# A row of a load split over 126 and 2 partitions: in the sixth load instead of the second

## The chip, the core and the metric

The kernel runs on one core of a Trainium2 chip. The metric is the device time of one execution in microseconds, taken over several executions. The engines that matter here are DVE (VectorE), ACT (ScalarE) and SP (SyncE), and the 16 DMA engines of the core, which move data between HBM and SBUF.

## The reference: what is computed

A softmax with temperature 2 over the last axis of a tensor of 16 x 1024 x 512 float32 values (33.55 MB in, 33.55 MB out):

```python
x_scaled = x / 2.0
x_max = np.max(x_scaled, axis=-1, keepdims=True)
exp_x = np.exp(x_scaled - x_max)
return exp_x / np.sum(exp_x, axis=-1, keepdims=True)
```

## The kernel before

The 16,384 rows of 512 values are dealt to 128 partitions, so each partition holds 128 rows of 2 KB. They are handled in ten tiles, t0 to t9, of 3, 7, 13 and seven times 15 rows per partition (`PLAN`, lines 11 to 14). One tile is one load and one store: each of the 128 partitions reads or writes one contiguous piece of 2 KB times the rows of the tile, so 6, 14, 26 and seven times 30 KB. A tile is computed in chunks of 3 to 5 rows.

All data lies in one SBUF buffer, the arena, of 98 rows per partition. Tiles t0 to t7 have places of their own; t8 and t9 take the places of t0 to t3, so their loads must wait until those tiles have been stored. Data is transformed in place.

- **Loads** (`issue_loads`, lines 98 to 114). SP issues the load of t0 (line 105). ACT issues those of t1 to t7 one after the other on its own DMA queue, without a wait: t1 ahead of the program's opening barrier, in the entry block (line 229), t2 to t7 behind the barrier. One tile, number `SPREAD`, is loaded by three DMAs (lines 108 to 112) where the others are loaded by one (line 114): all rows but the last over 128 partitions, then the last row for partitions 0 to 125, then the last row for partitions 126 and 127. The loads of t8 and t9 come later on the same queue, between ACT's computations (line 190), when the stores of t0 to t2, and of t3, have landed.
- **DVE** takes for each chunk the negated maximum (`do_max`, line 118), which waits for the tile's load: for 48 counts of its semaphore where the tile was loaded by three DMAs, for 16 otherwise (line 123). Two chunks later it forms the reciprocal of the sum (line 127) and multiplies the chunk with it, in one instruction for t1 to t3 (line 131) and row by row elsewhere (line 138). DVE's order is written out by hand: maximum of chunk k, then reciprocal and product of chunk k-2 (lines 149 to 153).
- **ACT** computes exp(0.5 x - max) row by row with the sum beside it (line 176; in a loop at line 211 for t6 to t9).
- **SP** issues the store of a tile when its last chunk is multiplied (line 158), in order of the tiles, and at the end waits for all stores (line 162).

The loads of t1 to t9 stand in one DMA queue (q10, ACT's) and the stores, with the load of t0, in another (q1, SP's). Both use the same 16 DMA engines. The lines that issue the loads and wait for them:

```python
elif t == SPREAD:
    r = tiles[t][1] - 1
    for p, q, lo, hi in ((0, P, 0, r), (0, 126, r, r + 1), (126, P, r, r + 1)):
        nc.scalar.dma_start(
            out=sb(t)[p:q, lo:hi], in_=dram(xf, t)[p:q, lo:hi]
        ).then_inc(ld[t], 16)
else:
    nc.scalar.dma_start(out=sb(t), in_=dram(xf, t)).then_inc(ld[t], 16)
...
)._wait_ge(ld[t], 48 if t == SPREAD else 16).then_inc(s_max, 1)
```

## Time and profile before

| | |
|---|---|
| median of 6 runs | 160.03 us (159.96 to 160.27) |
| the profiled execution | 160.17 us |
| its span, first to last instruction | 158.8 us |
| DVE busy | 131.4 us, 83% of the span |
| ACT busy | 94.4 us, 59% of the span |
| moved by DMA | 67.13 MB, 423 GB/s over the span |
| time of DMA packets, as a share of 16 engines' span | 50.4% (SP's queue) + 48.6% (ACT's queue) |

The span leaves out 1.37 us of the profiled execution's time, which lie around it. Times within the span are counted from its first instruction. A DMA is cut into packets, and each packet stands in the trace with its start, its length, its bytes and its queue; a packet of 4 bytes is the finishing write with which one DMA engine reports that its part of a DMA is done. "Landing" is the moment at which the last such report has reached the semaphore.

### The profile page before, as it was taken

The numbers are of one execution on the slowest core, as the hardware profiler recorded it, in microseconds if no ns is written. First come the engines' busy times: TensorE is split into PE (matmuls) and PEld (weight loads), VectorE is DVE, ScalarE is ACT, GpSimd is POOL, SyncE is SP. The second block draws the span as 40 slices with busy tenths as digits, with TensorE's granted clock in tenths as the row PEclk, the third lists the DMA queues.
The fourth block names the chain that finished last, engine by engine and source line by source line (L and its number), as shares of the span: only waits on it lengthen the run. The fifth ranks groups of instructions, "written<-read, shape, count | busy, mean of one in ns | idle before, by whom it ended". The sixth has DMA issues, their size and how long they took to land.

```text
span 158.8 us, 621 instructions
## 1 busy us (share of the span) xinstructions
DVE 131.4 (83%) x155; ACT 94.4 (59%) x257; POOL 0.2 (0%) x4
## 2 busy tenths in 40 slices
DVE  0466799999999999999999999994999479999100
ACT  0369187746784595668848697666566809664000
POOL 0000000000000000000000000000000000000000
DMA  7989999999998999999999999999999999999996
GB/s 283 441 365 429 439 430 441 433 406 414 451 430 387 448 462 424 441 420 449 418 441 418 449 418 449 418 449 410 457 410 457 410 457 410 457 410 449 418 449 263
DMA packets 3026, 67.13 MB, mean 423 GB/s; under 512 B 336, under 2 KB 336, under 8 KB 720
## 3 DMA queue, kind: packets, MB, share of 16 engines
q1 hardware_dynamic: 1584, 34.34, 50.4%
q10 hardware_dynamic: 1440, 32.77, 48.6%
q14 instruction: 2, 0.02, 0.0%
HBM read 33.55 MB, written 33.55 MB: 423 GB/s over the span
## 4 chain that ended last, share of the span: by engine, by line
DMA 53%; DVE 38%; issue 0%
DMA arena<-in_x_dram 39%; DVE stats L118 18%; DMA out_dram<-arena 14%; DVE arena L131 13%; DVE arena L138 7%; DVE recip L127 1%
## 5 line engine op out<-in xcount | busy, mean ns | idle before, releaser
L118 DVE TENSOR_REDUCE stats<-arena 128x5 f32<-128x2560 f32 (+2 forms) x27 | 72.2, 2676 | 15.0 <-DMA arena<-in_x_dram 15.0
L176 ACT ACTIVATE arena<-arena,stats 128x512 f32<-128x512 f32 x68 | 48.2, 710 | 23.4 <-DVE stats L118 23.4
L211 ACT ACTIVATE arena<-arena,stats x60 | 42.5, 709 | 21.3 <-ACTq L203 21.3
L138 DVE TENSOR_SCALAR arena<-arena,recip 128x512 f32<-128x512 f32 x93 | 38.6, 482 | 0.7
L131 DVE TENSOR_TENSOR arena<-arena,recip 128x2560 f32<-128x2560 f32 (+2 forms) x8 | 19.9, 2492 | 0.3
L176 ACT ACTIVATION_READ_ACCUMULATOR arena<-arena,stats 128x1 f32 x68 | 12.7, 187 | 0.0
L211 ACT ACTIVATION_READ_ACCUMULATOR arena<-arena,stats x60 | 11.2, 186 | 0.0
L127 DVE RECIPROCAL recip<-stats 128x5 f32<-128x5 f32 (+2 forms) x27 | 4.8, 177 | 0.0
L171 ACT ACT_TABLE_LOAD x1 | 1.3, 1283 | 5.7 <-issue 5.7
L252 POOL MEMSET const-uint8-127<- 128x1 uint8 x1 | 0.1, 103 | 0.0
L252 POOL MEMSET const-bfloat16-1.0<- 128x1 bf16 x1 | 0.1, 102 | 0.0
L252 POOL MEMSET const-float32-0.0<- 128x1 f32 x1 | 0.1, 99 | 0.2 <-issue 0.2
L252 POOL MEMSET const-float32-1.0<- 128x1 f32 x1 | 0.1, 99 | 0.0
## 6 DMA issues: line engine op xcount, KB each, us to landing
arena<-in_x_dram ACTq DMA_DIRECT2D x7, 3840.0 KB, 47.0
out_dram<-arena SPq DMA_DIRECT2D x7, 3840.0 KB, 22.4
arena<-in_x_dram ACTq DMA_DIRECT2D x1, 3328.0 KB, 14.2
out_dram<-arena SPq DMA_DIRECT2D x1, 3328.0 KB, 21.3
out_dram<-arena SPq DMA_DIRECT2D x1, 1792.0 KB, 17.5
arena<-in_x_dram ACTq DMA_DIRECT2D x1, 1536.0 KB
arena<-in_x_dram SPq DMA_DIRECT2D x1, 768.0 KB, 6.2
out_dram<-arena SPq DMA_DIRECT2D x1, 768.0 KB, 15.1
```

Source lines behind the costliest of these rows:

```text
L118: nc.vector.reduce_max(out=stats[:, b : b + c], in_=arena[:, a : a + c], axis=mybir.AxisListType.X, negate=True,)._wait_ge(ld[t], 48 if t ...
L127: nc.vector.reciprocal(out=recip[:, b : b + c], in_=stats[:, b : b + c])._wait_ge(s_exp, k + 1).then_inc(s_rec, 1)
L131: nc.vector.tensor_mul(out=arena[:, a : a + c], in0=arena[:, a : a + c], in1=recip[:, b : b + c].unsqueeze(2).to_broadcast([P, c, D]),)._w ...
L138: ins = nc.vector.tensor_scalar_mul(out=arena[:, a + r], in0=arena[:, a + r], scalar1=recip[:, b + r : b + r + 1],)
L171: nc.scalar.preload_act_table(mybir.ActivationFunctionType.Exp)
L176: ins = nc.scalar.activation(out=arena[:, a + r], in_=arena[:, a + r], func=mybir.ActivationFunctionType.Exp, bias=stats[:, b + r : b + r ...
L211: ins = nc.scalar.activation(out=data, in_=data, func=mybir.ActivationFunctionType.Exp, bias=stat, scale=0.5, accum_out=stat,)
L252: nc = _bacc.Bacc("TRN2", target_bir_lowering=False, num_devices=1)
```

## The change

```diff
-SPREAD = 1
+SPREAD = 5
```

The second load (t1, 7 rows per partition, 14 KB) becomes one DMA over 128 partitions. The sixth load (t5, 15 rows, 30 KB) becomes three: 14 rows (28 KB) over 128 partitions, then the last row over partitions 0 to 125, then the last row over partitions 126 and 127. The waits on the two semaphores change with it: 16 for t1, 48 for t5. On ACT two DMA issues move from the entry block, ahead of the barrier, to behind the issue of t4's load. No instruction of DVE, SP, PE or POOL changes its place.

## The prediction

> **What bounds the kernel now.** I first read the head of the page: span, engines, the slices, the DMA queues.

> ```profile
> span 158.8 us, 621 instructions
> DVE 131.4 (83%) x155; ACT 94.4 (59%) x257; POOL 0.2 (0%) x4
> ...
> DMA  7989999999998999999999999999999999999996
> ...
> DMA packets 3026, 67.13 MB, mean 423 GB/s; under 512 B 336, under 2 KB 336, under 8 KB 720
> ...
> q1 hardware_dynamic: 1584, 34.34, 50.4%
> q10 hardware_dynamic: 1440, 32.77, 48.6%
> ```

> The DMA engines are busy in every slice, and the two queues' shares sum to 99.0%: 157.2 us of packets on each of 16 engines. That is the bound; DVE has 27 us to spare. The chain of waits ends in DMA too:

> ```profile
> 58.69 22.37 DMA out_dram<-arena
> ...
> 81.08 46.98 DMA arena<-in_x_dram
> ...
> 128.09 2.82 DVE stats L118
> ```

> The 47 us of t9's load are mostly time in a queue, not a price. So I read where DVE waits for loads (timeline of DVE; in brackets the idle time ahead):

> ```profile
> 9.16 3.95 DVE L118 TENSOR_REDUCE stats<-arena 128x4 f32<-128x2048 f32 x2 [1.23 <-DMA arena<-in_x_dram]
> ...
> 16.87 2.82 DVE L118 TENSOR_REDUCE stats<-arena 128x5 f32<-128x2560 f32 x1 [2.37 <-DMA arena<-in_x_dram]
> ...
> 63.51 2.81 DVE L118 TENSOR_REDUCE stats<-arena 128x5 f32<-128x2560 f32 x1
> ...
> 109.95 2.82 DVE L118 TENSOR_REDUCE stats<-arena 128x5 f32<-128x2560 f32 x1 [1.99 <-DMA arena<-in_x_dram]
> ...
> 128.09 2.82 DVE L118 TENSOR_REDUCE stats<-arena 128x5 f32<-128x2560 f32 x1 [3.26 <-DMA arena<-in_x_dram]
> ```

> These are t1, t2, then t5 (its first chunk, no wait), t8 and t9. DVE is ahead of the loads again from 107.96 on.

> Last, the trace's packet records. They don't name the DMA engine, but on one engine a packet begins 4 ns before the one ahead of it ends, so they link into 16 rows. What they show:

> - From about 1.3 us to its end no engine is idle, but for a hole of 0.35 us at 45.3 and one of some 0.5 us at 140, one engine each. The 16 rows end between 157.58 and 158.32; the last report lands at 158.78.
> - One packet is one partition's piece: 1138 ns for 30 KB, 987 for 26 KB, 535 for 14 KB, 460 for 12 KB, 84 for 2 KB (80 from start to start). So 2 KB inside a long piece costs (1138 - 987)/2 = 75 ns.
> - A DMA over 128 partitions gives each engine 8 packets and one finishing write. ACT's queue has 1440 packets = 9 whole DMAs x 144, 128 single rows, and 16 finishing writes for the 126 and the 2 rows together: 126 rows on 14 engines, 9 each, and 2 on two of them. **Two engines get nothing of the split row.** They are the two that begin latest: at 7.65 they finish t1's 12 KB pieces (the others 6.93 to 7.41) and go straight on to t2; the fourteen take 9 rows and finish at 7.66 to 8.26.
> - Where both queues hold work, an engine takes them in turn, one packet of each, whatever the sizes.

> **The change, part by part** (against the profiled 160.17).

> *t1 in one piece.* The two engines have 8 x 75 = 0.60 us more: 7.65 becomes 8.25. The fourteen have 8 x 75 instead of 9 x 80 + 9 ns of finishing: 0.60 - 0.73 = 0.13 less, so the last at 8.26 becomes 8.13. t1 is complete at the same time.

> *t2.* The two engines ended it at 15.91 and 16.02, now 16.5 and 16.6; the fourteen (last 16.41) now 16.3. The load is complete 0.2 later; DVE waits there, so its first chunk of t2 moves from 16.87 to 17.05. DVE runs without a wait from there to 107.96, so stores t2 to t5 go out 0.2 later. The 1.99 us wait for t8 swallows it.

> *t5 in three pieces.* The long pieces lose 8 x 75 = 0.60 on all engines, and the fourteen gain 0.73. So **every engine's sum is what it was**: two engines +0.60 - 0.60, fourteen -0.13 + 0.13.

> *Order of the queues around t5.* Here stores run beside loads, and a row of 2 KB takes a turn like a piece of 30 KB. On a typical engine t5 was loaded at 55.08, and t2's store (26 KB pieces, first at 45.20) ended at 61.44. After: the eighth long piece (start 52.96 before) ends near 53.4, 0.73 earlier; four store pieces are done by then. Four remain and alternate with t5's finishing write and the first three rows: 53.4 + 4 x 0.99 + 3 x 0.08 = 57.6. Then the store queue is empty, and six rows follow bare, 0.5: t5 complete at 58.1, landing near 58.5 by the 0.4 us that other loads take from finishing write to report. DVE takes t5 at 63.7: 5.2 us of cover. If that cover were gone, each us would delay t4's store.

> *The next store.* t3's store is issued at 58.69, now 58.9. On engines busy with loads the first packet of a store came 3.69 (issue 14.54, packet 18.23), 4.5 (26.20, 30.71) and 3.56 us (41.64, 45.20) behind its issue. By that it begins at 62.5 to 62.8; before, behind t2's, at 62.3 to 62.6. As the engines never idle, the same bytes are moved by then, so t6's load stands where it stood too. From there on everything repeats: t8 and t9 land at 109.9 and 128.1.

> *ACT.* Three issues took 1.36 us ahead of the barrier; one long issue took 0.39. Behind the barrier the six issues (2.65 to 5.65) become eight, about 0.9 longer. If the barrier opens 0.9 sooner, nothing moves; if not, the table load (1.28) ends at 7.86, and the first exp at 7.97 still finds ACT free (its 1.01 us of idle time is the cover). Every long load is queued long before its turn. Both ends: zero.

> *The end.* The last store is issued at 147.40. The first packet of a DMA on idle engines came 1.02 behind its issue (SP's load at 0.00), so it could begin at 148.4; the last engine takes it up at 149.22. So t9's landing may be **0.8 us later before the end moves**, and an earlier landing brings nothing.

> *Not shown before.* (a) Rows between store pieces: 9 x 7 ns if they lose as 6 KB packets did between 12 KB ones (241 for 234), up to 9 x 92 = 0.8 by the slowest lone row (176 for 84). I take 0.06; six of nine run bare. (b) t2's first packet took 1.24 to 1.44 on all engines, not 0.99: 0.35 lost. Every later load but that begins at full rate. If the burst of rows causes it, it may go (-0.35); if the burst repeats it at t5 while another cause keeps it at t2, +0.35. I take 0: the two engines without rows lose it as well, which names no cause.

> [...] In this trace single pieces alternate.

> Sum: 160.17 + 0.06; against the median, 0.14 lower, **160.1**.

> **Rivals.**

> *Store one turn early (slower).* If t3's store begins at 61.4 instead of 62.5, all later loads are one piece (1.13) late. For it: the store queue now stands empty and waiting. Against it: a turn 2.4 to 3.0 behind the issue was passed by in all cases above, and 61.4 is 2.5 behind. Two engines that stood one turn the other way in this trace loaded t9 at 126.0 instead of 127.0 and ended no different, which shows the price: t9 lands at 129.2, 1.13 late, less 0.8 of cover, +0.35: 160.4. It decides once t9 lands after 128.9; with the upper end of (a) on top, 160.7.

> *The rows cost twice (slower).* (a) or (b) at the upper end, on engines that never idle, goes straight into the end: +0.35 to 0.8, 160.4 to 160.8.

> *The burst was the cause of the lost 0.35 (faster).* For it: the loss comes right behind the rows, and reports of that load took 0.9, not 0.4 us. Without it: 159.7.

> *Doesn't do what it says:* the order of instructions per engine shows the three DMAs at t5; excluded.

> **Numbers.** Forecast 0.50 (159.8 to 160.35); store one turn early 0.15; rows cost twice 0.13; burst gone 0.22. The two slower ones lie partly over the 0.2% line (0.32 us, about what a measurement of this kernel can tell from no change); I count them slower: 0.28, faster 0.22, same 0.50. Range: from the burst gone at 159.65 to the slower ones at 160.7.

> **What would show it.** Right: t1's maximum begins at 8.6 to 9.16; t2's maximum at 17.05; t5 landing at 58 to 59; a stretch from 58 to 62 in which loads alone are moved; t3's store beginning near 62.6; t9's maximum within 127 to 128.9; last landing at 158.8. Wrong: t2's first packets at 0.99 (the faster rival); t9's maximum beyond 128.9 (the first slower one); rows of over 0.1 us or a stretched first piece of t6 (the second). It all fails if turns aren't taken one packet each, or if an engine's sum changes in a way no row here shows.

## The result, and the profile after

The changed kernel takes 160.59 us (median of 17 runs, 160.34 to 160.88) against 160.06 us (37 runs, 159.96 to 160.27) of the kernel before: a ratio of 1.0034, 95% interval 1.0028 to 1.0041. It is slower by 0.53 us. The likeliest forecast, no change, did not come; the time lies in the range, among the two slower rivals. The profiled execution took 160.51 us, its span is 159.2 us.

The head of the page of the changed kernel, to be held against the lines of before:

```profile
span 159.2 us, 621 instructions
DVE 131.5 (83%) x155; ACT 94.4 (59%) x257; POOL 0.2 (0%) x4
...
DMA  7999998999999999999999999999999999989988
...
DMA packets 3026, 67.13 MB, mean 422 GB/s; under 512 B 336, under 2 KB 336, under 8 KB 720
...
q1 hardware_dynamic: 1584, 34.34, 50.4%
q10 hardware_dynamic: 1440, 32.77, 48.6%
```

Packets and bytes are the same, and the queues' shares have not changed to the digit. But they are shares of a span that is 0.4 us longer: summed from the packet records, an engine's packets take 157.61 us on the mean, against 157.31 before. The same bytes took 0.30 us more. New is also the end of the DMA row: its last five slices read 89988, where before they read 99996. The timeline of DVE, the lines that answer to those of before (idle time ahead in brackets; t1, t2, t5 without a wait, t8, t9):

```profile
8.51 3.94 DVE L118 TENSOR_REDUCE stats<-arena 128x4 f32<-128x2048 f32 x2 [0.36 <-DMA arena<-in_x_dram]
...
16.43 2.82 DVE L118 TENSOR_REDUCE stats<-arena 128x5 f32<-128x2560 f32 x1 [2.58 <-DMA arena<-in_x_dram]
...
63.08 2.81 DVE L118 TENSOR_REDUCE stats<-arena 128x5 f32<-128x2560 f32 x1
...
111.17 2.82 DVE L118 TENSOR_REDUCE stats<-arena 128x5 f32<-128x2560 f32 x1 [3.28 <-DMA arena<-in_x_dram]
...
129.32 2.82 DVE L118 TENSOR_REDUCE stats<-arena 128x5 f32<-128x2560 f32 x1 [3.27 <-DMA arena<-in_x_dram]
```

The start is better than before: t1 is taken 0.65 us sooner, t2 0.44, t5 0.43. From t8 on everything is later: t9 by 1.23 us. Somewhere between 63 and 111 the loads lost what they had won.

The packet records show where. In the kernel before, a typical engine ran t5's end without short rows; now thirteen of the fourteen engines run as worked out: four store pieces with three rows between them, six rows bare, t5's last finishing writes at 57.8 to 58.4, four pieces of t6 alone, and t3's store from 62.5 to 62.8. The DMA queues between 58.5 and 61.5, first of the changed kernel:

```profile
q10 hardware_dynamic: 39, 1.20, 92.7%
q1 hardware_dynamic: 4, 0.05, 4.2%
```

and of the kernel before:

```profile
q10 hardware_dynamic: 32, 0.98, 75.9%
q1 hardware_dynamic: 30, 0.43, 33.2%
```

The store queue (q1) has run empty; the few pieces left in it are those of the two engines without rows. One engine, however, one with a tenth row, comes out of its burst of rows at 58.35, 0.25 to 0.5 us behind the rest. Its turn falls at 61.90 instead of 61.4, 3.64 us behind the issue of t3's store, which the chain of waits shows at 58.26:

```profile
58.26 22.54 DMA out_dram<-arena
```

By then the store is there: the engine takes it after three pieces of t6, not four. From then on its loads are one piece late, and it ends t9's load at 128.85, where the other fifteen end at 126.94 to 128.00. All of DVE waits for that one engine.

The end, in stretches around the last two stores (DMA share and GB/s are the last two columns), of the changed kernel:

```profile
139.20:141.00 1.80, 1.80 (x2) 1.80 (x6) 0.00 (x0) 1.00 0.72 307
141.00:148.80 7.80, 7.50 (x19) 3.70 (x11) 0.00 (x0) 1.00 1.03 441
148.80:150.00 1.20, 0.00 (x0) 0.00 (x0) 0.00 (x0) 1.00 0.96 410
```

and of the kernel before:

```profile
139.20:141.00 1.80, 1.76 (x3) 0.62 (x2) 0.00 (x0) 1.00 1.19 512
141.00:148.80 7.80, 6.30 (x17) 3.64 (x10) 0.00 (x0) 1.00 0.98 421
148.80:150.00 1.20, 0.00 (x0) 0.00 (x0) 0.00 (x0) 1.00 1.19 512
```

A share over 1 comes from packets that are booked where they begin. Behind 139.2 most DMA engines now stand idle for a while: t8's store is issued at 139.3 instead of 138.1, t9's at 148.6 instead of 147.4. Sixteen engines then end within 0.16 us of each other (158.62 to 158.78; before 157.59 to 158.32): t9's store begins on all of them at 149.47 to 149.62, 0.83 to 0.98 us behind its issue.

That reads like a finished story: one early turn, t9 late, idle time at the end. The experiments show that it is half of it.

### The profile page after: what moved, and what is told of

Its sections match the earlier page's. It is cut to its first block, busy times and chain, and to the rows that moved or that the text cites. A ratio compares the mean times of both kernels' runs of the same rounds, so it can differ in the third digit from the quotient of the medians.

```text
span 159.2 us, 621 instructions
## 1 busy us (share of the span) xinstructions
DVE 131.5 (83%) x155; ACT 94.4 (59%) x257; POOL 0.2 (0%) x4
## 2 busy tenths in 40 slices
DMA packets 3026, 67.13 MB, mean 422 GB/s; under 512 B 336, under 2 KB 336, under 8 KB 720
## 3 DMA queue, kind: packets, MB, share of 16 engines
q1 hardware_dynamic: 1584, 34.34, 50.4%
q10 hardware_dynamic: 1440, 32.77, 48.6%
## 4 chain that ended last, share of the span: by engine, by line
DMA 54%; DVE 38%; issue 0%
DMA arena<-in_x_dram 40%; DVE stats L118 18%; DMA out_dram<-arena 14%; DVE arena L131 13%; DVE arena L138 7%; DVE recip L127 1%
## 5 line engine op out<-in xcount | busy, mean ns | idle before, releaser
L118 DVE TENSOR_REDUCE stats<-arena 128x5 f32<-128x2560 f32 (+2 forms) x27 | 72.2, 2676 | 16.2 <-DMA arena<-in_x_dram 16.2
```

The costliest lines, as they stand in the source:

```text
L118: nc.vector.reduce_max(out=stats[:, b : b + c], in_=arena[:, a : a + c], axis=mybir.AxisListType.X, negate=True,)._wait_ge(ld[t], 48 if t ...
```

## The experiments

Theory A is that story. Its rivals: the DMA work itself has grown (B), or the missing relief of two engines at t1 costs (C); "relief" is that two engines get no short row there and so carry less. Every experiment was timed over five rounds beside the kernel before.

**e1: DVE's order at the end.** In the changed kernel the products of t8's last two chunks go ahead of the maximum of t9's first chunk. Then t8's store need not wait for t9's load.

```diff
+            if k == len(chunks) - 3:
+                do_mul(k - 2)
+                do_mul(k - 1)
             if k < len(chunks):
                 do_max(k)
-            if k >= LAG:
+            if k >= LAG and k not in (len(chunks) - 3, len(chunks) - 2):
                 do_mul(k - LAG)
```

> The changed kernel; DVE alone is reordered at the end: the products of t8's last two chunks come ahead of the first maximum of t9, in the time in which DVE waits for t9's load anyway. No DMA changes. Theory A (the loss is idle time of the DMA engines at the end, because one engine took t3's store a turn early, t9 landed 1.2 us later and the last two stores were issued 1.2 us later): t9 still lands near 129.3, but the last stores are issued some 3 to 4 us before 148.6, no engine waits for them, and the time falls to 160.0 to 160.1. Rival B (the DMA work itself has grown, by rows between store pieces or by the late relief of two engines): 160.6 as before the reordering.

Measured: 160.53 us, ratio 1.0030 (1.0018 to 1.0042). The idle time is gone, as the same stretches show:

```profile
139.20:141.00 1.80, 1.76 (x6) 1.80 (x6) 0.00 (x0) 1.00 1.11 478
```

and so are its causes: the last stores are issued at 129.8 and 145.9 (139.3 and 148.6 without the reordering), and in this execution no engine took an early turn either (t9 loaded by 128.11 at the latest).

```profile
L161 SPq DMA_DIRECT2D out_dram<-arena x2: 332/332/333, 129.8 to 145.9; - x2
```

Yet the last engine ends at 158.77, and the span is 159.2 us as before the reordering. **Theory A falls as the sole cause.** The idle time is real, but a second bound stands at the same place: two engines that never wait at the end reach 158.68 and 158.77 by work alone. In the changed kernel's own trace two engines run through the end without a hole as well, to about 158.7.

**e2: the 2 rows first.**

```diff
-((0, P, 0, r), (0, 126, r, r + 1), (126, P, r, r + 1))
+((126, P, r, r + 1), (0, P, 0, r), (0, 126, r, r + 1))
```

> The changed kernel, with the DMA of the 2 rows issued ahead of the 14 rows of t5 instead of behind the 126 rows; same DMAs, bytes and engines. Theory A, in its narrow form (only the two engines with a tenth row come 0.4 us later out of the burst and so meet t3's store a turn earlier): all fourteen engines come out alike, t9's first maximum starts at 127.8 to 128.6, 160.0 to 160.2. If other engines meet the early turn too, or if the rows cost by themselves (B): 160.5 to 160.7.

Measured: 160.53 us, 1.0031 (1.0019 to 1.0042); t9's first maximum at 129.52. The narrow form falls: now two engines whose bursts ended at 58.2 and 58.6 met t3's store at 61.83 and 62.10. Which engine meets it is a matter of tenths of a us, not of the tenth row.

**e3 and e4: each half of the change alone.** e3 splits no load (`SPREAD = -1`); e4 splits t1 and t5.

```diff
-SPREAD = 5
+SPREAD = (1, 5)
...
-            elif t == SPREAD:
+            elif t in SPREAD:
```

> No load is split: the removal at t1 alone, without the split at t5. Two engines then carry 0.60 us more in all than in the kernel before, the fourteen 0.13 less. Theory A: those two engines ended at 157.6 before, so at 158.2 now, not behind the latest engine (158.3); no rows beside stores, t9 as before: 160.0 to 160.2, and t2's first pieces at 0.99 us without the lost 0.35. Rival C (the missing relief of the two engines is what costs): 160.6 or more.

> t1 and t5 are both split: the split at t5 alone, without the removal at t1. Fourteen engines carry 0.13 us more than in the kernel before, two 0.60 less. Theory A: the early turn at t3's store depends on the split at t5 only: t9's first maximum near 129.3 and 160.5 to 160.8. Rival C (it was the removal at t1): 160.1 to 160.2.

Measured: e3 160.28 us, 1.0010 (1.0001 to 1.0019); e4 160.37 us, 1.0022 (1.0013 to 1.0031). Against the 160.09 of their own runs of before: +0.19 for taking t1's split away, +0.28 for adding t5's, 0.47 together, and the change costs 0.53. Both halves cost, and they nearly add up. In neither did t9 come late (its first maximum in e3, then in e4), so no early turn was needed for it:

```profile
128.30 2.82 DVE L118 TENSOR_REDUCE stats<-arena 128x5 f32<-128x2560 f32 x1 [3.26 <-DMA arena<-in_x_dram]
...
128.44 2.82 DVE L118 TENSOR_REDUCE stats<-arena 128x5 f32<-128x2560 f32 x1 [3.27 <-DMA arena<-in_x_dram]
```

For e4 theory A had expected 129.3 and 160.5 to 160.8; both failed to come. In e3 the two engines that finish t1 last, at 8.3, also end last, at 158.66 and 158.68; for the two without relief 158.2 was expected.

**e5: DVE's order at the end, in the kernel before** (the diff of e1).

> The kernel before, with the same reordering of DVE at the end. In the kernel before no engine waited for the last two stores, so theory A expects no gain: 159.9 to 160.1. If the last store's issue at 147.40 was a bound there too, it would gain 0.2 or more.

Measured: 160.06 us, 0.9998 (0.9989 to 1.0007): no gain, as expected. There the issue of the last store was not a bound.

**e6: the split in t6** (`SPREAD = 6`).

> The split is in the seventh load, t6, where stores are always queued (t4's is issued at 73.5, before t3's is done). By turns of one packet each, nine rows give nine store pieces the way: the loads behind fall back by several pieces of 1.13 us, bounded by the stores that are there by the end of the loads (about three pieces more). Theory A: t9 lands 2 to 4 us later, and the time is 161 to 163. If the rows went in one turn, or their place did not matter: 160.1 to 160.6.

Measured: 165.25 us, 1.0293 (1.0250 to 1.0336), more than expected; the profiled execution took 164.22. The packet records show the turns: behind t6's long pieces, a row at 73.30, a store piece of 30 KB at 73.38, a row at 74.52, a store piece at 74.60. DVE's waits for loads in this kernel (t6, t7, t8, t9):

```profile
80.75 2.82 DVE L118 TENSOR_REDUCE stats<-arena 128x5 f32<-128x2560 f32 x1 [2.80 <-DMA arena<-in_x_dram]
96.76 2.82 DVE L118 TENSOR_REDUCE stats<-arena 128x5 f32<-128x2560 f32 x1 [1.13 <-DMA arena<-in_x_dram]
114.90 2.82 DVE L118 TENSOR_REDUCE stats<-arena 128x5 f32<-128x2560 f32 x1 [3.26 <-DMA arena<-in_x_dram]
133.05 2.82 DVE L118 TENSOR_REDUCE stats<-arena 128x5 f32<-128x2560 f32 x1 [3.27 <-DMA arena<-in_x_dram]
```

t9 is taken at 133.05, 5.0 us late. The bound in the expectation was too low: late loads make late stores, the store queue runs dry, and between 140 and 144 the DMA engines are mostly idle (their share is in the column before the last):

```profile
140.00:144.00 4.00, 3.96 (x8) 2.85 (x9) 0.00 (x0) 1.00 0.27 115
```

So the mechanism of theory A exists: where stores are in stock, the split costs 5.2 us, ten times what the change costs.

**e7: t5's rows ahead of its long pieces.**

```diff
-((0, P, 0, r), (0, 126, r, r + 1), (126, P, r, r + 1))
+((0, 126, r, r + 1), (126, P, r, r + 1), (0, P, 0, r))
```

> The changed kernel with the order of t5's three DMAs turned round: 126 rows, 2 rows, then the 14 long rows. The rows then run near 40 us beside t1's store (14 KB pieces) and not just ahead of t3's. Theory A: a loss of turns there is given back, since the store queue runs empty before t2's store anyway: 160.0 to 160.3. Rival B: 160.6.

Measured: 160.47 us, 1.0026 (1.0016 to 1.0036), with t9's maximum at 128.05 and no early turn. Between the two expectations, and for B.

**e8, e11, e12: the split in t2, t3, t4** (`SPREAD = 2`, `3`, `4`).

> The split is in the third load, t2, which ends at 16 us, before any store has begun (first store packet at 18.2). Theory A: no turn is lost: 160.0 to 160.2. If the relief of two engines had to come at the second load: 160.5.

> The split is in the fourth load, t3, whose end (26.5 to 27) runs beside the last pieces of t0's store (6 KB, 0.23 us each). By theory F a row there costs little, since the store pieces are short: 160.1 to 160.3. If only the lateness of the relief counts: between t2's 160.10 and t5's 160.59, about 160.3.

> The split is in the fifth load, t4, whose end (39.5) runs beside t1's store (14 KB pieces, 0.54 us). The rows stand at about the same time as those of the run with t5's rows first (160.47). Theory F: 160.3 to 160.5, and the first piece behind the second instruction fetch near 1.49 us. If it's t5's own place that costs: 160.1.

Measured: 160.10 us, 1.0003 (0.9994 to 1.0012); 160.30, 1.0013 (1.0004 to 1.0022); 160.45, 1.0024 (1.0014 to 1.0033). With t1's 160.06 and t5's 160.59 that makes a slope: the later the uneven split (126 rows on 14 engines, 2 rows on two of them, none on the other two), the dearer, well before stores are in stock. Held against no split at all (e3, 160.28), it gains about 0.2 us in t1 or t2, nothing in t3, and costs 0.2 to 0.3 us in t4 or t5. The times came as expected; the piece behind the fetch in e12 did not (1.615 us, see the table).

**e9 and e10: even splits.** The last row goes by one DMA over 128 partitions, without relief for any engine: in e9 t1's, in place of 126 and 2; in e10 t5's, with t1 split 126 and 2 as before. The edit of e9 (e10 issues the same two DMAs in a branch of its own for t5; the counts waited for are 32):

```diff
-((0, P, 0, r), (0, 126, r, r + 1), (126, P, r, r + 1))
+((0, P, 0, r), (0, P, r, r + 1))
```

> The kernel before, with t1's last row loaded by one DMA over 128 partitions instead of 126 and 2: the burst of short rows stays, the relief of two engines goes (they carry 0.65 us more, the fourteen 0.08 to 0.16 less). If what t1's split buys is the relief (theory D: without it two engines end last, as near 158.67 without any split): 160.2 to 160.4, like the kernel without a split (160.28). If it is the burst, which holds engines up once and spares later stretched pieces (theory E): 160.0 to 160.1.

> The kernel before (t1 split 126 and 2), with t5's last row loaded by a DMA of its own over all 128 partitions: rows beside t2's and t3's stores on all engines, no second relief; every engine carries 0.05 us more. If the cost of the split at t5 is the short rows between and behind store pieces (theory F): 160.3 to 160.6, as with both splits (160.37) or more. If it comes from the unevenness of 126 and 2: 160.1.

Measured: e9 160.02 us, 0.9997 (0.9988 to 1.0006): **t1's split does not work by the relief of two engines.** Theory D and rival C fall, though narrowly: the intervals of e9 and of e3 (1.0001 to 1.0019) still meet. Theory E has its number, but not its reason: in e9 the burst holds the engines up by 0.01 us only. Why an even row at t1 is worth 0.26 us against no split stays open. e10 160.19 us, 1.0007 (0.9998 to 1.0016), against 1.0022 for the uneven split in the same place (e4): the short rows by themselves cost 0.1 us or nothing, and most of t5's price comes with the uneven split. These two intervals also meet, and an uneven split differs from an even one in three things at once (two DMAs for the row, nine rows on an engine instead of eight, two engines without any), which no run separates. Theory F falls in the form in which it was put.

**What the runs have in common.** Three numbers of each profiled execution, from the packet records. "Stretched": by how much packets that begin from 7.4 to 62 us took longer than such packets mostly do, summed and divided by 16 engines. "Behind the fetch": near 71 us one engine moves a packet of 8 KB from the queue that the page calls instruction ("the fetch" here), 0.31 to 0.33 us; this is the length of the store piece that follows it, 1.138 elsewhere. "Last end": the last finishing write. e6, which loses its time elsewhere, is left out.

| run | split | stretched | behind the fetch | last end | median |
|---|---|---|---|---|---|
| before | t1 | 0.90 | 1.488 | 158.32 | 160.06 |
| e5 | t1 | 0.80 | 1.488 | 158.22 | 160.06 |
| e9 | t1 even | 0.83 | 1.492 | 158.33 | 160.02 |
| e8 | t2 | 0.82 | 1.488 | 158.31 | 160.10 |
| e10 | t1, t5 even | 0.74 | 1.505 | 158.34 | 160.19 |
| e3 | none | 1.00 | 1.494 | 158.68 | 160.28 |
| e11 | t3 | 1.01 | 1.488 | 158.50 | 160.30 |
| e4 | t1, t5 | 0.88 | 1.620 | 158.61 | 160.37 |
| e12 | t4 | 0.97 | 1.615 | 158.54 | 160.45 |
| e7 | t5, rows first | 0.97 | 1.612 | 158.55 | 160.47 |
| e1 | t5 | 1.16 | 1.620 | 158.77 | 160.53 |
| e2 | t5 | 1.25 | 1.620 | 158.99 | 160.53 |
| after | t5 | 1.13 | 1.620 | 158.78 | 160.59 |

The five runs with up to 0.90 and a short piece behind the fetch take 160.02 to 160.19; those with one of the two longer take 160.28 to 160.37; those with both take 160.45 to 160.59. This sorts the runs after the fact, by one execution of each; no run takes either term away alone, so it is not shown that they are the cause. From before to after the stretched time grows by 0.23 us on the mean of 16 engines, and the fetch engine alone loses 0.14 more (0.13 in the piece, 0.01 in the fetch). The two together would be 0.37 of 0.53, but a mean and one engine's loss do not add up to an account: on the fetch engine's own row the stretched time grows from 0.7 to 1.3 us, and part of that is won back by a start of t2 that is 0.49 us earlier (7.50 against 7.99). In before and e1 that engine is one of the two that end last, and in the changed kernel one of the two that run through without a hole. The other loses 0.57 us (before) and 0.6 to 0.8 us (e1, after) in small amounts of up to 0.05 us a piece, late in its row. The two had no slack in the kernel before, ending at 158.29 and 158.32 where the others had ended by 157.95, so whatever lengthens their row lengthens the kernel.

## Why the prediction was right or wrong

- **Bound, packets, turns, order of the queues: right.** Turns of one packet each, 14 engines with nine rows, t5 complete at 57.8 to 58.4 (58.1 worked out), loads alone until t3's store at 62.5 to 62.8: as put. DVE took t5 at 63.08 with cover to spare. One reading was off: the records of before have no hole of some 0.5 us at 140; the engine that ends last there loses that time in small amounts from 90 us on. In the changed kernel (on one engine rows at 55.13 and 56.20, store pieces at 55.21 and 56.28) and in e6 (rows at 73.30 and 74.52, store pieces at 73.38 and 74.60) single rows alternate with single pieces.
- **ACT: right.** The load of t2 is issued at 1.58 instead of 2.65, the table load begins at 5.69 instead of 5.68.
- **"Every engine's sum is what it was": the step that failed.** The mean of the 16 sums grew by 0.30 us, from 157.31 to 157.61 (157.33 in e3, 157.47 in e4). The step counted packets at their usual lengths and took 0 for (b), the stretched packets. I had seen 0.35 us lost behind t1's rows and could not say what takes its place without them. The runs do: with an uneven split in t1 or t2, 0.35 to 0.45 us are lost by 16.5 us and at most 0.04 from there to 28; without one, 0.10 at most by 16.5 (e9 included) and 0.31 to 0.48 after it. So an uneven burst moves the loss more than it makes one. It grew by 0.07 (0.42 to 0.49), by 0.04 between 28 and 56, and by 0.13 behind t5's rows, where t6's first pieces took 1.24 to 1.30 instead of 1.138: the stretch that I had asked of the second slower rival. That is also most of why t2 was taken at 16.43 and not at 17.05: the 0.35 behind t1's rows was gone, and only later came back.
- **The row that I had not:** the piece behind the instruction fetch. Its 1.488 was in the records of before, within the row of one of the two last engines, and I had not asked what the last engines owe their place to.
- **"Store one turn early": right in mechanism and in t9's landing, wrong in weight; its price is not shown.** Put at 129.2 for t9, it came at 129.32. The +0.35 cannot be read from the changed kernel: its packets end at 158.78 instead of 158.32, but in e1 they end at 158.77 without any late store. The turn at 61.4 was passed by as forecast, on thirteen engines; I had reckoned with a typical engine, and one engine that comes 0.4 us later is enough, since DVE waits for the last. It is not what the kernel loses by, though: e1 takes it away and gains 0.06 us, within the intervals of both.
- **"The rows cost twice": right in sign**, by uneven DMAs more than by short rows. The rows themselves kept their 84 ns between store pieces. That 0.53 lies within the 0.35 to 0.8 put is partly luck: t6's first pieces lost 0.13, not 0.35, and 0.19 of the cost comes from taking t1's split away (e3), which this rival did not have. So it is also luck that the time fell into the range: its slower end stood there for other reasons.
- **"The burst gone, faster": half right.** The loss at t1 vanished, DVE came 0.44 us sooner, and none of it reached the end.

Open stays why a DMA on 14 and 2 engines stretches the packets of all 16 when an even one does not; why the fetch engine's piece takes 1.61 to 1.62 us in just those kernels whose uneven rows run between 39 and 59 us; and the up to 0.5 us, in e8 0.7 and in e6 2.5, by which single runs of one kernel differ.

## What to carry to other kernels

Here the DMA engines are busy almost from start to end, and the span ends 0.4 to 0.5 us behind the last engine's last packet (158.32 of 158.8 us before, 158.78 of 159.2 after). Where that is so, link the packets of each engine, see which end last and by which packets, and put every edit against those, not against the mean. A bound that is seen to be new (idle time, a late load) is the cause only if the time comes back when it is taken away; here two bounds had come to the same place. A page whose shares stand still while the span grows says that the work has grown (here 50.4% and 48.6% in both, of 158.8 and 159.2 us). A DMA of 2 KB rows cost turns where the other queue was in stock (in e6 a row at 73.30, a store piece of 30 KB at 73.38): the same split was free in the third load (e8, 160.10 us), which ends by 16.4 us, ahead of the first store packet (18.23, both in the kernel before), and cost 5.2 us in the seventh (e6, 165.25).
